# Routing of a mixture-of-experts layer: splits on one engine, the norm's root ahead of the last rows, the gates' table ahead of the gathered rows, two experts in a written order

## The chip, the core and the metric

One core of a Trainium2 chip runs the kernel. Its engines run side by side and wait for each other by semaphores: TensorE (PE) multiplies matrices, VectorE (DVE) and ScalarE (ACT) work on whole tiles, GpSimd (POOL) works on tiles and issues the transfers with computed addresses, SyncE (SP) issues most plain transfers. The metric is the device time of one execution in microseconds.

## The reference

A decoder layer with 1024 tokens of width 1024. A mixing part and a cross-attention to a memory come first, and both add to `x`. Then comes the mixture of experts, with which this document deals: of 4 groups with 8 experts each a token takes the best group, and in it the two best experts.

```python
pg = softmax(t @ w_rg + b_rg); gate_g, gidx = top_k(pg, 1)
el = (t @ w_re + b_re).reshape(N, 4, 8)[arange(N), gidx]
pe_top, eloc = top_k(softmax(el), 2)
wts = gate_g * pe_top / sum(pe_top)
# for each expert e and the rows xb that chose it
y = (silu(xb @ w_gate[e]) * (xb @ w_up[e])) @ w_down[e]
out = einsum('nk,nkd->nd', wts, y)
x = x + out;  return rms_norm(x, norm_final)
```

`t` is the RMS norm of `x`, with the gain `norm_ffn`. All is float32.

## The kernel before, in words

**Products in three terms.** A float32 operand is split into a high part (`whi`, a cast on ACT, L285) and a low part (`wlo`, the difference, L286). A product is three matrix products: high by high (L141), low by high (L142), high by low (L143).

**The weights' stream.** `plan` lists all weight tiles in the order of their use, 512 KB each. `pump()` loads tiles on SP's queue up to `ahead["load"]` tiles ahead of the use, and splits them up to `ahead["split"]` tiles ahead. `take()` hands out the next tile and calls `pump()`. An expert uses 12 tiles: 4 of `w_gate`, 4 of `w_up`, 4 of `w_down`. While experts run the load is 30 and 31 tiles ahead, from expert 16 on only 10 (`LF`, `EF`). Raw tiles, their halves, the gathered rows, `y` and more share one pool of 45 buffers (`unit`). A scheduler deals them out, by its own simulation, when the program is built; a tile that gets a buffer waits for whoever used it before.

**The end of the memory stage (`mem_out`, `tail`, `mem_end`).** The tokens lie in two halves (`hf`) and the features in 8 slices (`f`). For each slice `fin` adds the last product to `x2`, and `tail` multiplies `x2` into the routing logits (`plg`), transposes it (`pt`), writes the rows times gain (`rowg`, DVE) and the plain rows (`rows`, ACT), and stores both from ACT's queue, to `td` (read by the gathers) and `x2d` (to which the experts add). After the last slice `rsq` computes the norm's root from `plg`, in 11 small DVE instructions (L157 to L165).

**Routing (`route`).** DVE finds the group and the experts, PE counts ranks (L1113 to L1118), DVE builds one-hot matrices (`Rb`, `R`, `V`), PE turns them into the list of tokens of each expert (`idx`, L1146 and L1152). POOL then issues the gathers of experts 0, 1 and 2 (`xg<-td,idx`). A second product, `table` (L1182, 16 matrix instructions), gives the gates `tab`; for `hf == 1` it is put off (`late`).

**Experts.** `x_t(e)` transposes the gathered rows on PE (`px`) and splits them (`xth` on ACT, `xtl` on DVE). `gate_up(e)` is 48 products with 512 columns, `h_t(e)` four transposes and a split (`ht`), `down(e)` 24 products and the scaled copy `y`; POOL adds `y` to `x2d` by a scatter with addition (L1415). `down(e - 1)` runs in the turn of expert `e`. Ahead of expert 0 stand `x_t(0)`, the gather of expert 3, the table and a count of blocks (8 small products, L1425, and 14 small DVE instructions, L1428 to L1435), which only the rare overflow blocks need.

**Order.** SP and POOL run in the order of the code throughout. PE, DVE and ACT are in code order from the last slice to the end of `route`; after that the scheduler orders them.

Of the kernel before, what the change touches and what calls it, by code (L numbers as in the profile page):

```python
# [12 lines left out]
AF = mybir.ActivationFunctionType  # L13
OP = mybir.AluOpType
AX = mybir.AxisListType
# [4 lines left out]
D = 1024  # L20
KT = 8
H = 512
NE = 32
# [22 lines left out]
RM = {mybir.EngineType.DVE, mybir.EngineType.PE, mybir.EngineType.Activation}  # L46
# [24 lines left out]
PS = 4  # L71
# [43 lines left out]
def tile_layer(tc, a, out):  # L115
    nc = tc.nc
# [7 lines left out]
    mm = nc.tensor.matmul  # L124
# [6 lines left out]
    def half(name, shape=(128, H), dt=F32):  # L131
        return up.tile(list(shape), dt, name=name, tag="v", bufs=NV)

    def ps1(name="ps"):
        return psum.tile([128, 512], F32, name=name, tag="ps", bufs=4)
# [877 lines left out]
        for i in range(2):  # L1013
            nc.gpsimd.memset(Mb[i][:, 0:3], 0.0)

    late = []

    def load_gfb():
        gfb["t"] = unit("gfb", [128, D])
        row(gfb["t"], a["norm_ffn_row"], D)  # L1020
# [22 lines left out]
    def route(hf, pl, store):  # L1043
# [105 lines left out]
        if hf == 0:  # L1149
            nc.vector.tensor_scalar(tabi, pt[:, :NE], 8192.0, None, op0=OP.add)  # L1150
        else:
            tt(idx, tabi, pt[:, :NE], op=OP.add)  # L1152
            for e in range(NX):
                gather(e)
            store(x2d, KT - 1)
            ahead["lo"] = nc.vector
        gs = tl("gs", N)
        red(gs, ge, axis=AX.X, op=OP.add)
        gate = tl("gate", N)
# [28 lines left out]
                tt(tf, tf, pt[:, :64], op=OP.add)  # L1188

        if hf:  # L1190
            late.append(table)
        else:
            table()
            yield 1.8, 0.0
# [8 lines left out]
    def mem_out(hf):  # L1203
        hs = slice(hf * H, (hf + 1) * H)
        plg = ps1("plg")
        rows = [None, None]

        def store(dst, f, i=0):
            nc.scalar.dma_start(dst[hs, (f - 1) * 128:(f + 1) * 128].rearrange("(t p) c -> p t c", p=128), rows[i])

        def zero_mm(start, stop):
            mm(plg[:, :168], oneb[0:1], bc(Mb[0][0:1, 0, None, 0:28], [1, 6, 28]), start=start, stop=stop)


        zero_mm(True, False)
        pend = []

        def logit(f, x2):
            for t in range(4):
                mm(plg[:, t * 36:t * 36 + 36], x2[:, t * 128:(t + 1) * 128], wr[:, f], start=False, stop=False)  # L1220

        def tail(f, x2):
            fs = slice(f * 128, (f + 1) * 128)
            if f < KT - 1:
                logit(f, x2)
            else:
                logit(f, x2)
                for t in range(4):
                    mm(plg[:, 160 + 2 * t:162 + 2 * t], acc["x2", hf][1][:, t * 128:(t + 1) * 128], ones[:, 0:2],
                       start=False, stop=False)  # L1230
                zero_mm(False, True)
            pt = ps1("pt")
            for t in range(4):
                nc.tensor.transpose(pt[:, t * 128:(t + 1) * 128], x2[:, t * 128:(t + 1) * 128], ident)

            if f % 2 == 0:
                rows[0] = unit("rows", [128, 4, 256])
                rows[1] = unit("rowg", [128, 4, 256])
            cs = slice((f % 2) * 128, (f % 2 + 1) * 128)
            p3 = pt.rearrange("p (t c) -> p t c", t=4)  # L1240
            tt(rows[1][:, :, cs], p3, bc(gfb["t"][:, None, fs], [128, 4, 128]), op=OP.mult)
            nc.scalar.copy(rows[0][:, :, cs], p3)
            if f % 2:
                store(td, f, 1)
                if not (hf and f == KT - 1):
                    store(x2d, f)
            if f == KT - 1:
                rsq(r3[:, 4 * hf:4 * hf + 4], plg[:, 160:168:2], D, 1e-6, "r")

        def fin(f, p, x2):  # L1250
            tt(x2, x2, p, op=OP.add)
            colsum(("x2", hf), x2, f)
            if pend:
                tail(*pend.pop())
            pend.append((f, x2))

        grp = {}
        todo = [(f, 0, 8) for f in range(KT)]
        if hf == 0:
            todo = [(0, 0, 6), (1, 0, 6), (0, 6, 8), (1, 6, 8)] + todo[2:]  # L1260
        for f, k0, k1 in todo:
            if k0 == 0:
                x2 = half("x2")
                nc.sync.dma_start(x2, x1d[f * 128:(f + 1) * 128, hs])
                if hf:
                    ahead["load"] += PF
                grp[f] = (take(), ps1("pp"), x2)
            (wh, wl), p, x2 = grp[f]
            for k in range(k0, k1):
                if k == 6:  # L1270
                    for x in until(("om", 3, hf)):
                        yield x
                if (f, k) == (7, 5):
                    for t in range(4):
                        mm(plg[:, 160 + 2 * t:162 + 2 * t], acc["x2", hf][0][:, t * 128:(t + 1) * 128], ones[:, 0:2],
                           start=False, stop=False)
                o = om[k, hf]
                mm3(p, wh[:, k], wl[:, k], o[:, 0], o[:, 1], k == 0, k == KT - 1)
                if k in (1, 3, 5):
                    yield 1.28, 0.0  # L1280
            if k1 == 8:
                fin(f, p, x2)
                yield 1.28, 0.0
        for k in range(KT):
            om.pop((k, hf))
        fini[hf] = (lambda: tail(*pend.pop())), plg, store
        done.add(("mo", hf))

    def mem_end(hf):
        for x in until(("mo", hf)):  # L1290
            yield x
        last, plg, store = fini[hf]
        if hf:
            man = tc.manual_schedule(engines=RM)
            man.__enter__()
        else:
            yield 0.0, 0.8
        last()
        if hf:
            for i in range(NX):  # L1300
                xg.append(unit("xg", [128, D]))
                nc.gpsimd.memset(xg[i], 0.0)
            ahead["load"] += PG
            ahead["lo"] = nc.gpsimd
            ahead["split"] = PS
            pump()
        yield 2.0, 3.0
        for x in route(hf, plg, store):
            yield x
        if hf:  # L1310
            man.__exit__(None, None, None)
# [61 lines left out]

    hts = {}

    def gate_up(e):
        xh, xl = xts.pop(e)
        gu = []
        for w in range(2):
            p = ps1("pgu")  # L1380
            for q in range(4):
                wh, wl = take()
                for k2 in range(2):
                    k = 2 * q + k2
                    ks = slice(k * 128, (k + 1) * 128)
                    mm3(p, xh[:, ks], xl[:, ks], wh[:, k2], wl[:, k2], k == 0, k == KT - 1)
            gu.append(p)
        hh = half("hh")
        nc.scalar.activation(hh, gu[0], AF.Silu, scale=tab[:, 1, e:e + 1])
        nc.vector.scalar_tensor_tensor(hh, gu[1], tab[:, 1, e:e + 1], hh, op0=OP.mult, op1=OP.mult)  # L1390
        hts[e] = hh
# [10 lines left out]
    def down(e):  # L1402
# [8 lines left out]
        if e == NE - 1:  # L1411
# [4 lines left out]
                                     in_=y, in_offset=None, bounds_check=S - 1, oob_is_err=False,  # L1416
                                     compute_op=OP.add)

    x_t(0)
    gather(NX)  # L1420
    late[0]()
    op = ctx.enter_context(tc.tile_pool(name="ov", bufs=1))
    pc = ps1()
    for t in range(8):
        mm(pc[:, :NE], oneb, Mb[t // 4][:, 3 + t % 4], start=(t == 0), stop=(t == 7))  # L1425
    nb = op.tile([128, NE], F32, name="nb")
    t1 = op.tile([128, NE], F32, name="t1")
    nc.vector.tensor_scalar(nb, pc[:, :NE], 128.0, None, op0=OP.is_gt)  # L1428
    for j in range(2, 8):
        nc.vector.tensor_scalar(t1, pc[:, :NE], 128.0 * j, None, op0=OP.is_gt)  # L1430
        nc.vector.tensor_add(nb, nb, t1)
    nov = op.tile([128, 2], F32, name="nov")
    nc.vector.tensor_reduce(nov[:, 0:1], nb, axis=AX.X, op=OP.add)
    novi = op.tile([128, 1], I32, name="novi")
    nc.vector.tensor_copy(novi, nov[:, 0:1])  # L1435
    for e in range(NE):
        ahead["load"] = LF if e >= NE - EF else max(LE, LA - LD * e)
        if e >= NE - ES:
            ahead["split"] = LZ
        if e >= NE - ED:  # L1440
            down(e - 1)
        gate_up(e)
        if e + 1 < NE:
            x_t(e + 1)
        if e + 1 + NX < NE:
            gather(e + 1 + NX)
        if 0 < e < NE - ED:
            down(e - 1)
        h_t(e)
        if e == 4:  # L1450
            nr = nc.values_load(novi[0:1, 0:1], min_val=0, max_val=NOV - 1,
                                skip_runtime_bounds_check_because="2048 assignments leave at most 15 further blocks")
        if e == PK:
            gfin = unit("gfin", [128, D])
            row(gfin, a["norm_final"], D)
# [221 lines left out]
```

## Time and profile before

| What | us |
|---|---|
| median of 3 runs (1419.73 to 1422.47) | 1420.8 |
| the profiled execution's own time | 1421.64 |
| its span, from the first to the last instruction | 1419.9 |
| PE busy in it | 1324.5 |
| DVE busy in it | 1006.7 |
| ACT busy in it | 832.9 |
| last weight product of the memory stage, last slice's logits | until 770 |
| first product of expert 0 starts | 797.38 |
| last product of the weights ahead of the final norm | ends about 1388 |

Times within the span are counted from its start. An idle time in a row stands in square brackets, with what ended it. PE's span between about 770 and 797 is where routing leaves it nearly idle; the profile's row of the granted clock shows 0.5 there.

### The profile page before, as it was taken

The page shows a single profiled execution, that of the slowest core. Times are in us where ns is not written, and L with a number is a line of the kernel's source. Part 1 is how long each engine was busy: PE and PEld are TensorE (multiplying, and loading weights), DVE is VectorE, ACT ScalarE, POOL GpSimd, SP SyncE. Part 2 cuts the span into 40 slices and gives each one's busy share as a digit, 9 for nine tenths or more (in the row PEclk, how much of TensorE's full clock was granted, in tenths as well). Part 3 has the DMA queues.
Part 4 walks back from the last instruction along what each step waited for, and adds up shares of the span by engine and source line. Part 5 has one row for each costly group of instructions (what it writes and reads, how often), then busy time and mean ns, then how long its engine had stood idle before and what let it go on. Part 6 is the DMA issues. An engine that isn't in the chain of part 4 may idle for free.

```text
span 1419.9 us, 20537 instructions
## 1 busy us (share of the span) xinstructions
PE 1324.5 (93%) x7420; PEld 1147.9 (81%) x7420; DVE 1006.7 (71%) x1593; ACT 832.9 (59%) x1136; POOL 263.9 (19%) x289
## 2 busy tenths in 40 slices
PE   7889999999999999999997799999989999999980
PEld 5889898989887889999886578888778888888860
DVE  6746685667856444333365778999879999999975
ACT  7524563455545553333222478888868888888863
POOL 3231210311112331112114101111111111111012
PEclk9989999999999999999998799999999999999995
DMA  8540211212275665013699599999999699999985
GB/s 308 157 133 1 60 45 60 83 45 46 82 241 184 203 230 180 16 46 102 231 329 336 189 325 356 363 355 357 354 369 349 241 369 381 371 355 370 369 285 205
DMA packets 103225, 322.39 MB, mean 227 GB/s; under 512 B 15747, under 2 KB 23971, under 8 KB 103120
## 3 DMA queue, kind: packets, MB, share of 16 engines
q1 hardware_dynamic: 76896, 272.14, 52.3%
q0 software_dynamic: 17776, 40.51, 10.3%
q10 hardware_dynamic: 8448, 8.39, 1.7%
q8 instruction: 59, 0.97, 0.3%
q14 instruction: 46, 0.38, 0.1%
HBM read 287.10 MB, written 46.66 MB: 235 GB/s over the span
## 4 chain that ended last, share of the span: by engine, by line
PE 69%; DMA 15%; DVE 7%; issue 5%; ACT 3%; POOL 1%; SPq 0%; POOLq 0%; ACTq 0%; DVEq 0%
PE pp L141 11%; PE pp L142 11%; PE pp L143 11%; PE pgu L142 5%; PE pgu L143 5%; PE pgu L141 5%; DMA raw<-in_w_gate 4%; DMA raw<-in_w_down 4%; DMA raw<-in_w_up 3%; PE py L141 3%; PE py L143 3%; PE py L142 3%; PE px L1369 1%; DVE wlo L286 1%; DMA x2d<-y,idx 1%
## 5 line engine op out<-in xcount | busy, mean ns | idle before, releaser
L286 DVE TENSOR_TENSOR wlo<-raw,whi 128x1024 fp32r<-128x1024 f32 (+1 forms) x467 | 553.9, 1225 | 87.0 <-ACT whi L285 77.4
L285 ACT CAST whi<-raw 128x1024 fp32r<-128x1024 f32 (+1 forms) x469 | 471.9, 1049 | 67.3 <-PE pgu L142 11.0
L141 PE MATMUL pgu<-whi,xth 128*128 128x512 f32 x512 | 198.5, 396 | 6.1 <-ACT whi L285 6.1
L142 PE MATMUL pgu<-wlo,xth 128*128 128x512 f32 x512 | 201.5, 394 | 1.4 <-DVE wlo L286 1.4
L143 PE MATMUL pgu<-whi,xtl 128*128 128x512 f32 x512 | 201.1, 393 | 0.3 <-DVE xtl L147 0.3
L1415 POOL DMA_INDIRECT x2d<-y,idx x31 | 49.6, 1600 | 462.8 <-ACT y L1414 419.4
L141 PEld LDWEIGHTS pgu<-whi,xth 128*128 128x128 f32 x512 | 97.0, 189 | 27.6 <-ACT whi L285 8.2
L142 PEld LDWEIGHTS pgu<-wlo,xth 128*128 128x128 f32 x512 | 96.9, 189 | 22.9 <-DVE wlo L286 2.3
L143 PEld LDWEIGHTS pgu<-whi,xtl 128*128 128x128 f32 x512 | 97.0, 189 | 20.6 <-DVE xtl L147 0.7
L141 PE MATMUL py<-whi,ht 128*128 128x512 f32 x256 | 102.4, 400 | 4.8 <-ACT whi L285 2.5
L142 PE MATMUL py<-wlo,ht 128*128 128x512 f32 x256 | 103.6, 405 | 0.4 <-DVE wlo L286 0.4
L143 PE MATMUL py<-whi,ht 128*128 128x512 f32 x256 | 101.1, 395 | 0.0
L639 ACT ACTIVATE p<-p,stt 128x128 f32<-128x128 f32 (+7 forms) x64 | 49.6, 776 | 49.9 <-DVE stt L638 40.7
L142 PE MATMUL pp<-wlo,hTh 128*128 128x256 f32 x256 | 73.1, 285 | 1.5 <-DVE wlo L286 1.5
L141 PE MATMUL pp<-whi,hTh 128*128 128x256 f32 x256 | 73.5, 287 | 0.2 <-ACT whi L285 0.2
L141 PE MATMUL pp<-whi,h2h 128*128 128x256 f32 x256 | 73.1, 285 | 0.0
L143 PE MATMUL pp<-whi,hTl 128*128 128x256 f32 x256 | 72.9, 285 | 0.0
L142 PE MATMUL pp<-wlo,h2h 128*128 128x256 f32 x256 | 72.5, 283 | 0.0
L143 PE MATMUL pp<-whi,h2l 128*128 128x256 f32 x256 | 72.5, 283 | 0.0
L141 PE MATMUL pp<-hTh,whi 128*128 128x512 f32 x160 | 64.4, 403 | 0.4 <-ACT ot L691 0.4
L143 PE MATMUL pp<-hTh,wlo 128*128 128x512 f32 x160 | 63.5, 397 | 0.0
L142 PE MATMUL pp<-hTl,whi 128*128 128x512 f32 x160 | 63.5, 397 | 0.0
(361 smaller groups left out, 2963.4 us busy)
## 6 DMA issues: line engine op xcount, KB each, us to landing
raw<-in_w_gate SPq DMA_DIRECT2D x128, 512.0 KB
raw<-in_w_up SPq DMA_DIRECT2D x128, 512.0 KB
raw<-in_w_down SPq DMA_DIRECT2D x128, 512.0 KB
raw<-in_w_in SPq DMA_DIRECT2D x19, 512.0 KB
raw<-in_w_kv_mem SPq DMA_DIRECT2D x16, 512.0 KB
raw<-vwd SPq DMA_DIRECT2D x16, 512.0 KB
raw<-in_w_q_memT SPq DMA_DIRECT2D x8, 512.0 KB
raw<-in_w_out SPq DMA_DIRECT2D x8, 512.0 KB
```

Of the source, the lines that this page charges most:

```text
L141: mm(o, sh, mh, start=start, stop=False)
L142: mm(o, sh, ml, start=False, stop=False)
L143: mm(o, sl, mh, start=False, stop=stop)
L285: nc.scalar.copy(hi[:, c], raw[:, c])
L286: ahead.get("lo", nc.vector).tensor_tensor(lo[:, c], raw[:, c], hi[:, c].bitcast(F32), op=OP.subtract)
L639: nc.scalar.activation(pe[:, :nk], pe[:, :nk], AF.Exp, bias=stt[:, 2 + m:3 + m], scale=slopes[hd], accum_out=stt[:, 4 + m:5 + m])
L1369: nc.tensor.transpose(px[:, k * 128:(k + 1) * 128], x[:, k * 128:(k + 1) * 128], ident)
L1415: nc.gpsimd.indirect_dma_start(out=x2d[:, :], out_offset=bass.IndirectOffsetOnAxis(ap=idx[:, e:e + 1], axis=0), in_=y, in_offset=None, bou ...
```

## The change

Five edits, in `tail`, `mem_end`, `route` and the start of the expert loop:

- `rsq` runs as soon as the logits are complete, ahead of the last slice's transposes. For the last slice of the second half ACT makes a copy of `x2` scaled by the gain (`x2g`), PE transposes this copy first and `x2` after it, and ACT writes both results; DVE's multiplication is gone there.
- The setting that sent the low parts to POOL (`ahead["lo"]`) goes; DVE does all. The four-tile-ahead split is raised at the end of `route`, not at its start.
- `table()` runs at the end of `route`, ahead of `x_t(0)`.
- The order of PE, DVE and ACT stays as written through experts 0 and 1. There `h_t(0)` stands between the two products of `gate_up(1)`.
- The count of blocks moves behind expert 1.

```diff
-            ahead["lo"] = nc.vector
...
         if hf:
-            late.append(table)
+            ahead["split"] = PS
+            pump()
+            table()
...
+            if f == KT - 1:
+                rsq(r3[:, 4 * hf:4 * hf + 4], plg[:, 160:168:2], D, 1e-6, "r")
...
+            if hf and f == KT - 1:
+
+                x2g = half("x2g")
+                nc.scalar.activation(x2g, x2, AF.Copy, scale=gffn[:, f:f + 1])
+                nc.scalar.copy(rows[1][:, :, cs], turned(x2g))
+                store(td, f, 1)
+                nc.scalar.copy(rows[0][:, :, cs], turned(x2))
+                return
+            p3 = turned(x2)
             tt(rows[1][:, :, cs], p3, bc(gfb["t"][:, None, fs], [128, 4, 128]), op=OP.mult)
...
-            if f == KT - 1:
-                rsq(r3[:, 4 * hf:4 * hf + 4], plg[:, 160:168:2], D, 1e-6, "r")
...
             ahead["load"] += PG
-            ahead["lo"] = nc.gpsimd
-            ahead["split"] = PS
             pump()
...
             gu.append(p)
+            if w == 0 and between:
+                between()
...
+    man = tc.manual_schedule(engines=RM)
+    man.__enter__()
     x_t(0)
     gather(NX)
-    late[0]()
...
-        gate_up(e)
+        gate_up(e, between=(lambda: h_t(0)) if e == 1 else None)
...
-        h_t(e)
+        if e:
+            h_t(e)
+        if e == 1:
+            man.__exit__(None, None, None)
+            count_blocks()
```

`turned(x)` is the four transposes that stood there before; `count_blocks()` holds the count as it was.

On DVE, at the last slice and the root, before (`x_7412` is the last slice's `x2`, `w_r` the root's scratch):

```order
L286 TENSOR_TENSOR wlo<-raw,whi 128x1024
L1241 TENSOR_TENSOR rowg<-pt,gfb 128x4x128
L1251 TENSOR_TENSOR x_7412<-x_7412,pp 128x512
L1241 TENSOR_TENSOR rowg<-pt,gfb 128x4x128
L157 TENSOR_SCALAR w_r<-plg 128x4
L158 TENSOR_SCALAR w_r<-w_r 128x4
L161 SCALAR_TENSOR_TENSOR w_r<-w_r 128x4
```

and now:

```order
L286 TENSOR_TENSOR wlo<-raw,whi 128x1024
L1253 TENSOR_TENSOR rowg<-pt,gfb 128x4x128
L1260 TENSOR_TENSOR x_7412<-x_7412,pp 128x512
L157 TENSOR_SCALAR w_r<-plg 128x4
L158 TENSOR_SCALAR w_r<-w_r 128x4
L161 SCALAR_TENSOR_TENSOR w_r<-w_r 128x4
```

The last `rowg` multiplication, which waits for transposes, no longer stands ahead of the root. POOL's two low parts of this place now stand on DVE behind `R`.

On PE, from the token lists to the first product of expert 0, before (`Rb` and `R` are the one-hot matrices, `px` the gathered rows turned, `cb` the ones of the count):

```order
L1146 MATMUL ps<-V,Rb 128x32
L1362 MATMUL px<-ident,xg 128x128 x8
L1182 MATMUL ps<-V,R 128x64 x8
L1425 LDWEIGHTS cb
L1425 MATMUL ps<-Mb_102,cb 128x32
```

and now:

```order
L1144 MATMUL ps<-V,Rb 128x32
L1179 MATMUL ps<-V,R 128x64 x8
L1369 MATMUL px<-ident,xg 128x128 x8
L141 MATMUL pgu<-whi,xth 128x512
L142 MATMUL pgu<-wlo,xth 128x512
```

The table stands ahead of the gathered rows, and nothing is left between these and the first product.

On ACT, in the turn of expert 2, with buffer numbers and waits, before (`y_7989` is expert 0's `y`; its scatter with addition signals `DMASW4`):

```order
L285 CAST whi_8029<-raw_7418 128x1024 [waits DVE_49,PE_49]
L285 CAST whi_8041<-raw_7420 128x1024 [waits DMAHW6_49,DVE_49]
L1389 ACTIVATE hh_8100<-pgu_8002,tab_96 128x512 [waits PE_49]
L285 CAST whi_8054<-raw_7518 128x1024 [waits DMAHW7_49,DMASW4_49]
L285 CAST whi_8066<-raw_7520 128x1024 [waits DMAHW0_49,PE_49]
```

and now:

```order
L285 CAST whi_8039<-raw_7418 128x1024 [waits DVE_49]
L285 CAST whi_8051<-raw_7420 128x1024 [waits DMAHW6_49,DVE_49]
L1398 ACTIVATE hh_8110<-pgu_8012,tab_96 128x512 [waits PE_49]
L285 CAST whi_8064<-raw_7525 128x1024 [waits DMAHW7_49]
L285 CAST whi_8076<-raw_7527 128x1024 [waits DMAHW0_49,PE_49]
```

The cast of the eighth tile no longer waits for expert 0's scatter: the buffers are dealt out another way. The buffer of expert 0's `y` now goes to `raw_8062`, a load for expert 4 on SP's queue.

## Rows read from the trace of the kernel before

**Rows 1.** Chain of waits, late experts: start us, us, what.
```profile
1250.37 0.23 PE py L142
...
1250.71 14.40 DMA raw<-in_w_gate
```
**Rows 2.** Table by stretches: stretch, length, busy times, clock, DMA share, GB/s.
```profile
771.00:778.00 7.00, 0.42 (x4) 0.26 (x3) 6.62 (x12) 2.48 (x3) 4.63 (x2) 0.50 1.01 348
```
**Rows 3.** PE in order of time, routing: start us, us, instruction, idle before.
```profile
769.63 0.32 PE L1212 MATMUL plg<-Mb,cb 1*128 1x168 bf16 x1
...
792.08 1.94 PE L1362 MATMUL px<-ident,xg 128*128 128x128 f32 x8 [5.56 <-DMA xg<-td,idx]
793.81 3.52 PE L1182 MATMUL ps<-V,R 128*128 128x64 f32 x16
...
797.38 0.77 PE L141 MATMUL pgu<-whi,xth 128*128 128x512 f32 x1
...
798.80 0.63 PE L141 MATMUL pgu<-whi,xth 128*128 128x512 f32 x1
...
800.08 0.44 PE L141 MATMUL pgu<-whi,xth 128*128 128x512 f32 x1
```
**Rows 4.** DVE in order of time, routing and count.
```profile
771.64 0.15 DVE L157 TENSOR_SCALAR w_r<-plg 128x4 f32<-128x4 f32 x1
...
773.21 0.16 DVE L161 SCALAR_TENSOR_TENSOR w_r<-w_r 128x4 f32<-128x4 f32 x1
773.41 2.32 DVE L162 TENSOR_TENSOR w_r<-w_r 128x4 f32<-128x4 f32 x1
775.76 2.26 DVE L165 SCALAR_TENSOR_TENSOR r<-w_r 128x4 f32<-128x4 f32 x1
...
788.55 1.22 DVE L1173 TENSOR_TENSOR R<-ra,rk 128x1024 f32<-128x1024 f32 x1
...
797.68 0.18 DVE L1430 TENSOR_SCALAR t<-ps 128x32 f32<-128x32 f32 x1
```
**Rows 5.** POOL in order of time, routing and first experts.
```profile
773.37 4.63 POOL L286 TENSOR_TENSOR wlo<-raw,whi 128x1024 fp32r<-128x1024 f32 x2 [7.94 <-ACT whi L285]
787.58 1.14 POOL L1039 DMA_INDIRECT xg<-td,idx  x1 [9.57 <-DVE wsel L1164]
...
834.30 1.36 POOL L1039 DMA_INDIRECT xg<-td,idx  x1 [0.31 <-issue]
```
**Rows 6.** ACT's queue in order of time: the last store to `td`.
```profile
771.77 0.37 ACTq L1209 DMA_DIRECT2D td<-rowg  x1
```
**Rows 7.** Tile `td`, 690 to 830 us, 12 transfers.
```profile
DMA to landing us min/median/max: 4.1/4.8/7.5
```
**Rows 8.** Tiles `xth` and `xtl` in the experts: ns min/median/max, first and last start.
```profile
L146 ACT CAST xth<-px x31: 999/1008/1020, 810.9 to 1351.7; 128x1024 fp32r<-128x1024 f32 x31
L147 DVE TENSOR_TENSOR xtl<-px,xth x31: 1214/1217/1226, 811.9 to 1353.0; 128x1024 fp32r<-128x1024 f32 x31
```
**Rows 9.** PE in order of time, experts.
```profile
813.18 0.50 PE L143 MATMUL pgu<-whi,xtl 128*128 128x512 f32 x1 [0.31 <-DVE xtl L147]
...
843.08 0.50 PE L141 MATMUL pgu<-whi,xth 128*128 128x512 f32 x1 [2.88 <-ACT whi L285]
...
866.26 0.39 PE L142 MATMUL py<-wlo,ht 128*128 128x512 f32 x1
```
**Rows 10.** ACT in order of time, experts 2 and 3.
```profile
841.98 3.89 ACT L285 CAST whi<-raw 128x1024 fp32r<-128x1024 f32 x4 [4.43 <-DMA x2d<-y,idx]
...
863.28 1.06 ACT L285 CAST whi<-raw 128x1024 fp32r<-128x1024 f32 x1 [0.58 <-PE pgu L142]
865.00 1.05 ACT L285 CAST whi<-raw 128x1024 fp32r<-128x1024 f32 x1 [0.66 <-DMA x2d<-y,idx]
```
**Rows 11.** Table by stretches, behind PE's stop at 843.
```profile
844.00:848.00 4.00, 3.97 (x10) 3.07 (x11) 3.83 (x5) 3.58 (x4) 0.00 (x0) 0.57 0.85 314
```
**Rows 12.** What SP's queue waited for, 1085 to 1120: us, times, longest.
```profile
SPq L276 <- DVE wlo L286: 19.8, 5, 16.5
```

More of the change, by code (lines that the diff above doesn't have):

```diff
@@ L1014, in small_consts @@
             nc.gpsimd.memset(Mb[i][:, 0:3], 0.0)
-    late = []
     def load_gfb():
@@ L1231, in tail, with turned @@
                 zero_mm(False, True)
-            pt = ps1("pt")
-            for t in range(4):
-                nc.tensor.transpose(pt[:, t * 128:(t + 1) * 128], x2[:, t * 128:(t + 1) * 128], ident)
+            if f == KT - 1:
+                rsq(r3[:, 4 * hf:4 * hf + 4], plg[:, 160:168:2], D, 1e-6, "r")
+            def turned(x):
+                pt = ps1("pt")
+                for t in range(4):
+                    nc.tensor.transpose(pt[:, t * 128:(t + 1) * 128], x[:, t * 128:(t + 1) * 128], ident)
+                return pt.rearrange("p (t c) -> p t c", t=4)
             if f % 2 == 0:
@@ L1239, in tail @@
             cs = slice((f % 2) * 128, (f % 2 + 1) * 128)
-            p3 = pt.rearrange("p (t c) -> p t c", t=4)
+            if hf and f == KT - 1:
[6 more added lines that the diff above has]
+            p3 = turned(x2)
             tt(rows[1][:, :, cs], p3, bc(gfb["t"][:, None, fs], [128, 4, 128]), op=OP.mult)
@@ L1244, in tail @@
                 store(td, f, 1)
-                if not (hf and f == KT - 1):
-                    store(x2d, f)
-            if f == KT - 1:
-                rsq(r3[:, 4 * hf:4 * hf + 4], plg[:, 160:168:2], D, 1e-6, "r")
+                store(x2d, f)
         def fin(f, p, x2):
@@ L1374, in tile_layer, with gate_up @@
     hts = {}
-    def gate_up(e):
+    def gate_up(e, between=None):
         xh, xl = xts.pop(e)
@@ L1417, in down, with count_blocks @@
                                      compute_op=OP.add)
+    man = tc.manual_schedule(engines=RM)
+    man.__enter__()
     x_t(0)
     gather(NX)
-    late[0]()
     op = ctx.enter_context(tc.tile_pool(name="ov", bufs=1))
-    pc = ps1()
-    for t in range(8):
-        mm(pc[:, :NE], oneb, Mb[t // 4][:, 3 + t % 4], start=(t == 0), stop=(t == 7))
     nb = op.tile([128, NE], F32, name="nb")
     t1 = op.tile([128, NE], F32, name="t1")
[L1428 to L1431, printed above, removed]
     nov = op.tile([128, 2], F32, name="nov")
-    nc.vector.tensor_reduce(nov[:, 0:1], nb, axis=AX.X, op=OP.add)
     novi = op.tile([128, 1], I32, name="novi")
-    nc.vector.tensor_copy(novi, nov[:, 0:1])
+    def count_blocks():
+        pc = ps1()
+        for t in range(8):
+            mm(pc[:, :NE], oneb, Mb[t // 4][:, 3 + t % 4], start=(t == 0), stop=(t == 7))
+        nc.vector.tensor_scalar(nb, pc[:, :NE], 128.0, None, op0=OP.is_gt)
+        for j in range(2, 8):
+            nc.vector.tensor_scalar(t1, pc[:, :NE], 128.0 * j, None, op0=OP.is_gt)
+            nc.vector.tensor_add(nb, nb, t1)
+        nc.vector.tensor_reduce(nov[:, 0:1], nb, axis=AX.X, op=OP.add)
+        nc.vector.tensor_copy(novi, nov[:, 0:1])
     for e in range(NE):
```

## The prediction

> **What bounds the kernel now.** I read the chain of waits from its end backwards first. From 1250 us on it runs through transfers of weights, and at 1250.71 it turns into a product of an expert's `w_down` [rows 1]: late loads start when a product gives up a buffer, so an earlier PE makes them earlier. Further back, in the experts, products follow each other every 0.23 us [rows 1], and an expert's 72 take some 17 us. PE sets the pace there, with few stops. That leaves two things to look at: those stops, and the stretch in which PE stands for want of lists. For this I read PE, DVE, POOL and ACT in order of time between 770 and 798. PE's last logits end at 769.95, its gathered rows come at 792.08, expert 0 starts at 797.38 [rows 3], and the clock granted in the beginning of this stretch is 0.50 [rows 2]. The chain runs over DVE (root, ranks, lists), POOL (gather), a transfer and PE. Whatever shortens it moves everything behind, loads included.
>
> The sum is made against the profiled execution's 1421.64 us; the median of the runs is 1420.8, which is 0.84 less. About 0.2%, 2.8 us, is what a measurement of this kernel can tell from no change.
>
> **The change part by part.** *The root ahead.* DVE starts the root at 771.64 [rows 4], since the last `rowg` multiplication stands ahead of it and waits for transposes. The logits are there at 769.63 + 0.32 = 769.95 [rows 3]. With that multiplication gone the root starts at about 770.0: **-1.6**. What took its place (a scaled copy, a second turn, two ACT copies) lies on ACT and PE, which have nothing else to do till the ranks. What hides it is judged below, at the store of `td`.
>
> *Low parts on DVE alone.* Two of the root's small instructions last 2.32 and 2.26 us, their neighbour on the same tile 0.16 [rows 4]. Just then, from 773.37, POOL makes two low parts in 4.63 us, 2.3 each [rows 5]. The long ones stood for as long as one of POOL's. On DVE's own queue low parts can't do that: (2.32 - 0.16) + (2.26 - 0.16) = **-4.3**. The two low parts now lie behind `R`, 2 x 1.22 us (the length of `R`, of the same shape [rows 4]). Nothing there waits for them before the first product, and DVE is idle meanwhile.
>
> Together -5.9: the first gather goes from 787.58 [rows 5] to 781.7, the end of `R` from 788.55 + 1.22 = 789.77 [rows 4] to 783.9.
>
> *The table ahead of the gathered rows.* Before, 792.08 to 797.38 are 5.3 us from the first turned rows to the first product, with the table's 3.52 within [rows 3]. The rows would now be there at 792.08 - 5.9 = 786.2, but the table starts with `R`, at 783.9, and ends at 787.4: it holds the rows up by 1.2. Behind it only the first half of the turn (some 1.0 of its 1.94 [rows 3]), its cast (half of 1.008 [rows 8]) and handovers remain, 2.0 in all. First product at 787.4 + 2.0 = 789.4 instead of 797.38: **-8.0** for the three edits together, -2.1 of it from the table. The low clock of the first products I leave as it was: products get short at 800.08 [rows 3], 8 us behind the first turn and 2.7 behind the first product, and PE now starts its table 5.5 us ahead of expert 0, nearly as the 5.3 before.
>
> *The written order of experts 0 and 1.* The scheduler had mixed the turn of expert 1 and `h_t(0)` between products; PE waited 0.31 us for `xtl` [rows 9]. In the written order nothing stands between the turn of expert 1 and its first product: PE waits for `xth`, 1.0 us and a handover, 1.1, and after two products for `xtl`, 1.22 less 0.46 [rows 8, 1], 0.75. That is 1.85 - 0.3 = **+1.5** (0 if the scheduler's mix cost as much elsewhere; 1.7 more if the clock falls).
>
> *The count behind expert 1.* 14 DVE instructions of 0.18 [rows 4], 2.5 us, and eight products of under 0.1 us now stand in expert 1 or 2, where the scheduler fits them between; before, they lay where DVE had little else. **+0.5** (0 to +2.8).
>
> *The buffers.* In the turn of expert 2 ACT waited 4.43 us for expert 0's scatter [rows 10]; PE stood 2.88 for the cast behind it [rows 9] and went on at a clock of 0.57 for 4 us [rows 11], which loses 4 x 0.43 = 1.7. The new deal of buffers lets that cast wait for its load alone: -2.88 - 1.7 = **-4.6** (0 to -5). That buffer now goes to a load for expert 4. SP will stand at it till the scatter lands, about as long as ACT would have stood and a little more, 7 us; some 30 tiles of lead cover it, and if they don't, that is the first rival.
>
> The deal turns against the kernel in two places. In expert 3's turn the first tile of `w_down`, cast at 863.28, now waits for expert 1's scatter, as the second does at 865.00 [rows 10]. PE needs that tile's low part about when it now multiplies it, 866.26 [rows 9]; cast and low part end at 865.0 + 1.05 + 1.22 = 867.3 and a handover later, so **+1.2**. One more such wait appears in the turn of expert 14, behind expert 12's scatter: **+1.2** again (each 0 to +3.4, the upper end with 1.7 for the clock as above). The last norm I leave at 0 (-1 to +1.5).
>
> Sum: -8.0 + 1.5 + 0.5 - 4.6 + 1.2 + 1.2 = -8.2. From 1421.64 that is 1413.4, and against the median **1412.6**. With the smaller terms at either end I hold 1409.5 to 1415.5 for this case.
>
> **The rivals.** *The stream takes the buffers' part back.* SP's queue now stands 7 us, and the faster experts use 4.6 us of the stream's slack. The slack shows where the lead is cut at expert 16: 16.5 us of waiting in one piece [rows 12]. That is more than 11.6, which speaks against it; that transfers are close to full beside expert 2 (0.85 [rows 11]) speaks for it. Then the 4.6 come back: 1417.2.
>
> *Slower: the clock.* The written order makes PE stop for 1.1 and 0.75 us at the start of expert 1, and no other work fills it. A stop of 2.88 took the clock to 0.57 [rows 9, 11]. If PE, coming out of routing, doesn't rise to the full clock before these stops and falls again at them, its 72 products up to expert 1's `up` part run 0.43 apart, as the three from 798.80 to 800.08 [rows 3], not 0.23. The first six, up to 800.08, did so before. (72 - 6) x 0.2 = +13.2: 1425.8. It decides from the point at which stops this short count as the long one did. In its favour is only that PE did start low before; against it, that its products got short 2.7 us behind the first.
>
> The Trainium skill ("TensorE: Matmul & The Clock Gate", section "A second HAM failure mode: psum-queue depth-cycling") speaks for this rival: it tells of a kernel in which frequent short idle times between groups of products, none of them long, made the clock swing. By it the time would be this rival's, 1425.8. No row above shows such short stops in a series, so the trace neither agrees nor speaks against it.
>
> *The gather gains nothing.* The last store to `td` is issued at 771.77 [rows 6] and now, behind two ACT copies, at about the same time. Transfers there land after 4.8, at most 7.5 us [rows 7], so at 779.3, 2.4 ahead of the new gather. All engines of the DMA are busy there (1.01 [rows 2]). With a landing of 12 us the gather would wait 2.4: 1415.0, and 1 us for each further one.
>
> *Better.* The two new waits and the written order cost nothing: 1412.6 - 3.9 = 1408.7.
>
> **How the numbers follow.** Forecast 0.62; stream 0.13, of which 0.05 beyond 1418.0; gather 0.07; better 0.08; the clock 0.05; several small terms at their dear ends, about 1418 to 1420, 0.05. Range: 1407.0 to 1418.0, which leaves out the clock, the dear ends and part of the stream's. Faster by over 0.2% (below 1418.0): 0.62 + 0.08 + 0.07 + 0.08 = 0.85. Within 0.2%: 0.10. Slower: 0.05.
>
> **What would show it.** In the new trace: the root's start near 770.0 and all its instructions near 0.16; the first gather near 781.7; table ahead of turn, first product near 789.4; PE idle some 1.1 and 0.75 at expert 1's start, clock full behind it; no stop at expert 2's eighth tile; in the turns of experts 3 and 14 stops of about 1 us that end with a cast behind a scatter; SP idle at expert 16 for less than 16.5. It is wrong if the gather waits for `td`, if DVE's long instructions stay long without POOL, or if PE waits for loads.

## The result, and the profile after

| | before | changed |
|---|---|---|
| median, us | 1420.8 (5 runs, 1416.82 to 1422.47) | 1409.82 (5 runs, 1408.05 to 1411.39) |
| span of the profiled execution | 1419.9 | 1408.1 |
| first product of expert 0 | 797.38 | 789.12 |
| last expert product ends (its start and 0.23, the step from product to product) | 1387.75 | 1379.67 |
| from there to the end of the span | 32.15 | 28.43 |

The changed kernel takes 0.992 of the time of the kernel before (95% interval 0.9907 to 0.9932). That is faster by more than 0.2%, inside the range of 1407.0 to 1418.0, and 2.8 us below the predicted 1412.6. One run of the kernel with the root alone (below) took 1683.64 us at a granted clock of 0.741, and no number here contains it.

The routing came out as in the sum, almost to the tenth. DVE in order of time (start us, us, instruction, idle before), which answers to [rows 4]:

```profile
769.99 0.16 DVE L157 TENSOR_SCALAR w_r<-plg 128x4 f32<-128x4 f32 x1 [2.45 <-PE plg L1211]
...
770.58 0.16 DVE L162 TENSOR_TENSOR w_r<-w_r 128x4 f32<-128x4 f32 x1
770.78 0.16 DVE L165 SCALAR_TENSOR_TENSOR w_r<-w_r 128x4 f32<-128x4 f32 x1
...
782.57 1.22 DVE L1170 TENSOR_TENSOR R<-ra,rk 128x1024 f32<-128x1024 f32 x1
783.71 2.35 DVE L286 TENSOR_TENSOR wlo<-raw,whi 128x1024 fp32r<-128x1024 f32 x2
```

The root starts 0.04 behind the last logits, all its steps last 0.16, and the two low parts lie behind `R`. POOL, against [rows 5]:

```profile
781.67 1.14 POOL L1037 DMA_INDIRECT xg<-td,idx  x1 [15.95 <-DVE wsel L1161]
783.12 1.57 POOL L1037 DMA_INDIRECT xg<-td,idx  x1 [0.30 <-issue]
```

And PE, against [rows 3]:

```profile
783.94 3.65 PE L1179 MATMUL ps<-V,R 128*128 128x64 f32 x16 [3.32 <-DVE R L1170]
787.38 1.92 PE L1369 MATMUL px<-ident,xg 128*128 128x128 f32 x8
789.12 0.76 PE L141 MATMUL pgu<-whi,xth 128*128 128x512 f32 x1
789.71 0.40 PE L142 MATMUL pgu<-wlo,xth 128*128 128x512 f32 x1
```

No idle time stands between the table, the turn and the first product. But the second product is already at its short length; before, six were slow. The experts, against [rows 9]:

```profile
802.56 0.50 PE L141 MATMUL pgu<-whi,xth 128*128 128x512 f32 x1 [1.10 <-ACT xth L146]
...
803.82 0.50 PE L143 MATMUL pgu<-whi,xtl 128*128 128x512 f32 x1 [0.53 <-DVE xtl L147]
...
853.13 0.50 PE L141 MATMUL py<-whi,ht 128*128 128x512 f32 x1 [0.16 <-ACT whi L285]
...
854.39 0.50 PE L142 MATMUL py<-wlo,ht 128*128 128x512 f32 x1 [0.76 <-DVE wlo L286]
...
1032.23 0.79 PE L141 MATMUL pgu<-whi,xth 128*128 128x512 f32 x1 [2.26 <-ACT whi L285]
...
1033.50 0.80 PE L142 MATMUL pgu<-wlo,xth 128*128 128x512 f32 x1 [0.47 <-DVE wlo L286]
...
1058.75 0.50 PE L142 MATMUL py<-wlo,ht 128*128 128x512 f32 x1 [0.69 <-DVE wlo L286]
```

The stops at expert 1 are there, expert 2 has none, the two new waits stop PE at 853 and at 1058, and the old stop of expert 13 is still there. The first of the new waits is ACT's, for expert 1's scatter:

```profile
852.02 2.00 ACT L285 CAST whi<-raw 128x1024 fp32r<-128x1024 f32 x2 [2.54 <-DMA x2d<-y,idx]
```

The other one stands the same way at 1056.38, after 1.77 of waiting.

What the sum didn't hold is the end: the way from the last product to the end of the span is 3.7 shorter.

### The profile page after: what moved, and what is told of

Same layout as the page of the kernel before. It is cut to its first block, busy times and chain, and to the rows that moved or that the text cites. A ratio compares the mean times of both kernels' runs of the same rounds, so it can differ in the third digit from the quotient of the medians.

```text
span 1408.1 us, 20553 instructions
## 1 busy us (share of the span) xinstructions
PE 1325.6 (94%) x7424; PEld 1148.1 (82%) x7424; DVE 1001.1 (71%) x1594; ACT 833.9 (59%) x1138; POOL 262.0 (19%) x287
```

## The experiments

In the records PE's first expert product is a good mark; so is the way from the root's start on DVE to the first gather on POOL, since it doesn't depend on when the memory stage ended in that record. That way is 15.94 us in the kernel before and 11.68 in the changed one.

But for its second record the changed kernel didn't run beside the experiments; each has a ratio to the kernel before from its own session. By these ratios the late table (0.9939, 0.9923 to 0.9956), the count first (0.9939, 0.9922 to 0.9955) and the end without POOL (0.990, 0.9884 to 0.9917) can't be told from the changed kernel with certainty, since their intervals overlap its 0.9907 to 0.9932. What is said of these three rests on the positions in the traces.

**The low parts alone.** The kernel before, with the split raised behind `R` and no low part on POOL:

```diff
+            ahead["split"] = PS
+            pump()
             late.append(table)
...
-            ahead["lo"] = nc.gpsimd
-            ahead["split"] = PS
             pump()
```

> The kernel before with one edit: the two low parts of the routing stand on VectorE behind R, as in the changed kernel; root, table, order and count stay. Theory (the root's two long instructions stood for POOL's two low parts): all eleven instructions of the root take 0.16 to 0.2, the first gather is issued 4.3 earlier than in the kernel before, at about 783.3, the first product of expert 0 at about 793.1, the time falls by about 4.3, to 1416.5. Rival (the root's instructions are long for another reason, such as the transfers beside them): they stay at 2.3 and the time stays within 1 of 1420.8.

Median 1416.05, ratio 0.9962 (0.9948 to 0.9976). Root to gather 783.21 - 771.53 = 11.68, first product at 793.02. The two steps of 2.3 are gone with POOL's work: the theory stands, at 4.3 us.

**The low parts ahead of the routing.** As above, but the split stays where the kernel before has it:

```diff
-            ahead["lo"] = nc.gpsimd
```

> As the run before it, but the two low parts stand on VectorE between the root and the routing's first step, where the kernel before gave them to POOL. Theory: 4.3 of POOL's hindrance are saved and 2 x 1.22 of VectorE's own work are put in, so the first gather comes 1.9 earlier than in the kernel before, at about 785.7, and the time is about 1418.9, between the kernel before and the run with the low parts behind R. Rival: the saving is the same as in that run, 4.3, since VectorE has waits there to fill.

Root to gather 785.36 - 771.54 = 13.82. DVE's record shows why:

```profile
773.58 2.35 DVE L286 TENSOR_TENSOR wlo<-raw,whi 128x1024 fp32r<-128x1024 f32 x2
```

2.35 of DVE's own work stand on the chain in place of 4.3 of waiting, and the first product (795.26) is 2.12 earlier than before, as expected. So half of the edit's gain hangs on where the split was moved to. The median, 1416.66 (0.9971, 0.9958 to 0.9983), fell further than the 1418.9 of the theory and can't be told from that of the low parts alone. In the profiled execution the rest lies at the end of the kernel, which takes 29.6 from the last product instead of 32.15 (below).

**The root alone.** The kernel before, with `rsq` ahead of the transposes:

```diff
+            if f == KT - 1:
+                rsq(r3[:, 4 * hf:4 * hf + 4], plg[:, 160:168:2], D, 1e-6, "r")
             pt = ps1("pt")
...
-            if f == KT - 1:
-                rsq(r3[:, 4 * hf:4 * hf + 4], plg[:, 160:168:2], D, 1e-6, "r")
```

> The kernel before with one edit: the root stands ahead of the last rows' transposes and multiplication; POOL keeps its low parts. Theory (what collides with POOL's low parts is whatever small two-operand step of VectorE stands there at that time): the root starts at 770.0 and is short throughout, but instructions of the routing behind it now last about 2.3, twice; the multiplication of 0.7 stands behind the root, so the first gather is only 0.9 earlier, 786.7, and the time about 1420. Rival (only the root is hurt): the gather is 1.6 + 4.3 - 0.7 = 5.2 earlier, 782.4, and the time about 1415.6.

The root is short, and the long steps have moved on. DVE, then POOL:

```profile
773.61 2.16 DVE L1073 TENSOR_TENSOR r_ao<-r_ae,r_af 128x128 f32<-128x128 f32 x1
775.69 2.31 DVE L1073 TENSOR_TENSOR r_go<-r_ge,r_gf 128x16 f32<-128x16 f32 x1
```

```profile
773.28 4.69 POOL L286 TENSOR_TENSOR wlo<-raw,whi 128x1024 fp32r<-128x1024 f32 x2 [9.61 <-ACT whi L285]
```

Root to gather is 785.03 - 768.90 = 16.13, no shorter than before. What is hurt isn't the root but a DVE step that stands beside POOL's. That the root itself starts earlier shows against the last logits on PE:

```profile
768.54 0.32 PE L1212 MATMUL plg<-Mb,cb 1*128 1x168 bf16 x1
```

From their end to the gather it is 785.03 - 768.86 = 16.17, and it was 787.58 - 769.95 = 17.63 before: 1.5 of the 1.6 that the sum gives to the root. Median 1418.81 (0.9987, 0.9977 to 0.9997).

**The low parts back on POOL.** The changed kernel with that edit undone:

```diff
             store(x2d, KT - 1)
+            ahead["lo"] = nc.vector
...
-            ahead["split"] = PS
-            pump()
             table()
...
             ahead["load"] += PG
+            ahead["lo"] = nc.gpsimd
+            ahead["split"] = PS
             pump()
```

> The changed kernel with one edit undone: the routing's low parts are on POOL again, split at the place of the kernel before. Theory: two small instructions of VectorE between 773 and 779 last about 2.3 instead of 0.2 to 0.3, the first gather is issued at about 786.0 instead of 781.67, the first product of expert 0 at about 793.4 instead of 789.12, and the time is about 4.3 over the changed kernel's, 1414.1. Rival (the gain came from the root's place alone): the gather stays at 781.7 and the time at 1409.8.

DVE's long steps come back, on still other instructions:

```profile
773.47 2.32 DVE L1069 TENSOR_TENSOR r_ge<-r_ge,desc 128x16 f32<-128x16 f32 x1
...
776.02 2.19 DVE L1071 TENSOR_TENSOR r_ao<-r_ae,r_af 128x128 f32<-128x128 f32 x1
```

Root to gather 785.36 - 769.67 = 15.69, 4.0 more than in the changed kernel; median 1415.26, 5.4 more, against 4.3 in the theory. In the profiled execution slow products account for more than that difference: 1.0 at the start of expert 0 and 1.6 at expert 1 (below).

**The table late again.** The changed kernel with `table()` behind `x_t(0)`:

```diff
-            table()
+            late.append(table)
...
     gather(NX)
+    late[0]()
```

> The changed kernel with one edit undone: the table stands behind the turn of expert 0's rows again, in the written order. Theory: the rows come at about 786.2, their turn starts there, the table runs behind it and holds the first product to about 791.5 instead of 789.12; the first products are slow as in the kernel before (0.43 apart, six of them, 1 us in all); the time is about 2.4 to 3.4 over the changed kernel's, 1412.2 to 1413.2. Rival (the first products are fast whatever the order, since PE's work ahead of them lasts as long): only the 2.4 show.

Median 1412.37, 2.6 over the changed kernel. In PE's record the rows' turn comes first and the table holds the product up:

```profile
786.16 1.94 PE L1370 MATMUL px<-ident,xg 128*128 128x128 f32 x8 [5.61 <-DMA xg<-td,idx]
787.89 3.52 PE L1179 MATMUL ps<-V,R 128*128 128x64 f32 x16
791.16 0.77 PE L141 MATMUL pgu<-whi,xth 128*128 128x512 f32 x1
```

That is 2.04 by the first product; ten products were slow from there on. The rows came 786.16 - 781.62 = 4.5 behind the gather's issue, as before (792.08 - 787.58), so the gather didn't wait for the store of `td`.

**No written order.** The changed kernel without `manual_schedule` at experts 0 and 1:

```diff
-    man = tc.manual_schedule(engines=RM)
-    man.__enter__()
...
-            man.__exit__(None, None, None)
             count_blocks()
```

> The changed kernel without the written order of experts 0 and 1: the scheduler orders them, and deals the buffers anew. It puts the turns of experts 1 and 2 ahead of the first product of expert 0. Theory: PE then waits for the gather of expert 2, which lands at about 790, so that the first product comes at about 791.5 instead of 789.1; the stops of 1.10 and 0.53 at expert 1 are gone; the scatter of expert 0 holds a cast of expert 2 again and costs PE 3 to 4.6; the time is 1412 to 1416. Rival (the written order costs more than it gives, as my sum has it, +1.5): the time is about 1408.3.

Median 1419.68 (ten runs, 1416.9 to 1422.12), above the 1412 to 1416 of the theory: nearly the whole gain is gone. The profiled execution, with a span of 1415.2, is the fastest of the ten. PE:

```profile
790.86 1.10 PE L1376 MATMUL px<-ident,xg 128*128 128x128 f32 x8 [1.31 <-DMA xg<-td,idx]
791.71 0.48 PE L141 MATMUL pgu<-whi,xth 128*128 128x512 f32 x1
...
803.72 0.50 PE L141 MATMUL pgu<-whi,xth 128*128 128x512 f32 x1 [0.83 <-ACT xth L146]
...
805.39 0.50 PE L143 MATMUL pgu<-whi,xtl 128*128 128x512 f32 x1 [0.94 <-DVE xtl L147]
...
835.32 0.79 PE L141 MATMUL pgu<-whi,xth 128*128 128x512 f32 x1 [3.38 <-ACT whi L285]
```

The scheduler put the turns of experts 1 and 2 ahead of the first product, and PE waited for a gather that it didn't need yet. The stops at expert 1 are not gone, as the theory had it, and no shorter than in the written order, and expert 0's scatter holds a cast of expert 2 again. The rival falls: with the table early, the scheduler's order costs more than the written one. How much of it is order and how much the deal of buffers stays open, since both changed.

**The count first.** The changed kernel with `count_blocks()` ahead of the loop:

```diff
+    count_blocks()
     for e in range(NE):
...
             man.__exit__(None, None, None)
-            count_blocks()
```

> The changed kernel with one edit undone: the count of blocks stands ahead of expert 0 again, in the written order. The deal of buffers then lets a cast of expert 2 wait for expert 0's scatter again. Theory (the count itself is cheap, what counts is the deal): the first product comes at most 0.5 later than 789.12, PE stands about 2.9 at the eighth tile of expert 2 and runs slow for 4 us behind it, and the time is about 4 to 5 over the changed kernel's, 1414 to 1415. Rival (the count was the cost, on VectorE ahead of expert 0's low parts): PE stops in expert 0 for 2 to 3 and not in expert 2.

Median 1412.58, 2.8 over the changed kernel, less than expected. The first product is at 789.03, 19.43 behind the root's start against 19.13 in the changed kernel, so the count costs 0.3 there. Expert 2 stops again, by its deal of buffers. ACT, then PE:

```profile
835.95 3.90 ACT L285 CAST whi<-raw 128x1024 fp32r<-128x1024 f32 x4 [3.69 <-DMA x2d<-y,idx]
```

```profile
837.04 0.50 PE L141 MATMUL pgu<-whi,xth 128*128 128x512 f32 x1 [1.66 <-ACT whi L285]
...
837.99 0.49 PE L141 MATMUL py<-whi,ht 128*128 128x512 f32 x1 [0.45 <-ACT whi L285]
```

The mechanism holds, the size was smaller: 2.11 of standing instead of 2.9, and no slow stretch behind it. The profiled execution, 1415.09, is the slowest of the four; the clock fell in it behind the stops of expert 1.

**Buffers of its own for `y`.** Two, with 43 in the shared pool, and one, with 44:

```diff
-NU = 45
+NU = 43
...
-        y = unit("y", [128, D])
+        y = up.tile([128, D], F32, name="y", tag="y", bufs=2)
```

> The changed kernel with a change of its own: the experts' y has two buffers of its own, and the shared pool has 43 instead of 45, so that no cast of weights waits for a scatter. Theory: the stops of 0.92 in expert 3's turn, of 2.73 with a slow stretch behind in expert 13's and of 0.69 in expert 14's are gone, about 6 us in all, and the time is about 1404. Rival (two buffers less leave the loads too late): SP's waits grow, PE waits for loads, and the time is 1410 or more.

> The changed kernel with one buffer of its own for y and 44 instead of 45 in the shared pool, to part what the run with 43 mixed: no cast waits for a scatter, and one buffer less. Theory (with 43 the cost was the missing buffers, 0.6 an expert, and the late end of the memory stage, 2.2): half of that or none is left, the stops at experts 3, 13 and 14 are gone, and the time is between 1404 and 1414. Rival (any buffer less costs 0.6 an expert and more): 1418 or more.

1421.69 and 1435.71: no gain in either, as the rivals had it (1410 or more, 1418 or more). The stops behind scatters are gone and others came. What SP's queue waited for between 860 and 1080 (us in total, times, longest), in the changed kernel:

```profile
SPq L276 <- PE pgu L143: 20.8, 29, 1.2
...
SPq L276 <- DVE wlo L286: 5.5, 10, 0.9
```

and with 43 buffers:

```profile
SPq L276 <- PE pgu L143: 42.4, 37, 2.0
...
SPq L276 <- DVE wlo L286: 35.6, 38, 1.7
```

Both also end the memory stage later; the root starts at 772.24 and 773.25 instead of 769.99. Then loads wait for buffers to be given back. With 43 the theory's 6 us did come back, 0.9 at expert 3 and 5.7, with the slow stretch, at experts 12 and 13. But in every expert from 4 to 10 PE loses 0.6 on the way from its gate to its up products, and from 21 to 28 it loses 1.2 an expert. Why 44 and one come out worse than 43 and two isn't settled. There PE also stood for `hh` and `xtl` on DVE, up to 1.8 at a time, and one `y` had to wait 8.0 for the scatter ahead of it; the casts behind it on ACT stopped PE for 6.46.

**The end without POOL.** The changed kernel with DVE scaling all rows of the last norm:

```diff
-FP = (3, 5, 7)
+FP = ()
```

> The changed kernel with a change of its own at the end: the three multiplications by the final gain that GpSimd made for rows 3, 5 and 7 are gone, and VectorE scales these rows by root and gain in one step, as it does the others. Theory (GpSimd's tile-long steps hold VectorE's small steps of the last root for 2.3 each, at the end as in the routing): the two small steps of 2.31 are down to 0.16, 4.3 saved, against 3 x 1.27 of rows that VectorE now scales itself; from the last product's end to the end of the span 27 to 28.5 instead of 28.4, the time 1408 to 1410. Rival (these steps are long for another reason): they stay, and the time is 3 to 4 over the changed kernel's, 1413.

Median 1406.7 (0.990 of the kernel before), the lowest of all and below the 1408 to 1410 expected. At the end of the changed kernel POOL and DVE look like the old routing; POOL first:

```profile
1384.49 5.24 POOL L1626 TENSOR_TENSOR xf<-xf,gfin 128x1024 f32<-128x1024 f32 x2 [3.13 <-ACT xfs L1624]
```

```profile
1385.13 2.31 DVE L161 SCALAR_TENSOR_TENSOR w_f<-w_f 128x1 f32<-128x1 f32 x1
...
1387.44 2.31 DVE L157 TENSOR_SCALAR w_f<-rfin 128x2 f32<-128x2 f32 x1
```

Without POOL's steps the same part of DVE reads

```profile
1385.08 0.15 DVE L161 SCALAR_TENSOR_TENSOR w_f<-w_f 128x1 f32<-128x1 f32 x1
...
1385.22 0.16 DVE L157 TENSOR_SCALAR w_f<-rfin 128x2 f32<-128x2 f32 x1
```

and the end, from the last product, takes 25.89 instead of 28.43, though DVE scales three more rows. That is more than the theory's own sum, 4.3 less 3 x 1.27. DVE is done only 0.7 earlier (17.0 behind the last product instead of 17.7); the rest lies behind it, where the last scatter on POOL follows DVE's end by 3.7 instead of 5.5. The last two stores in between were issued 0.4 apart in the changed kernel and 1.2 apart here; no run tests whether that is why they took longer there.

**Both kernels again.** The same programs, for second records.

> The changed kernel as it is, for another record of the same program. Theory (when the clock rises in expert 0, and whether it falls at the stops of 1.10 and 0.53 at expert 1, changes from run to run of the same instructions): the first product starts at 789.1 again and PE stops again for 1.10 and 0.53, but the number of slow first products differs from 1, or a slow stretch of 3 to 4 us stands behind the stops. Rival (order and stops decide it): one slow product and no slow stretch, as in the first record. Time 1408 to 1412.

> The kernel before as it is, for another record. Theory (the order of VectorE's small steps at the end, which the build sets, makes the end long): three small steps of 2.3 to 2.5 behind the last product again, the last gathered rows' step 1.5 to 4 behind the last product, 29.5 to 32.5 from the last product to the end, against 28.4 in the changed kernel. Rival (the long end of the first record was an accident of its transfers): under 29.

1408.89 and 1420.36. In the second record of the changed kernel the first product is at 787.77, since the memory stage ended 1.3 earlier (the root starts at 768.66). The stops at expert 1 are again 1.10 and 0.53, but six products were slow at the start of expert 0, and the clock fell behind the stops. By stretches (length, busy times, granted clock, DMA share, GB/s), first record and second:

```profile
803.00:805.00 2.00, 1.48 (x7) 1.00 (x6) 2.00 (x3) 1.47 (x3) 0.00 (x0) 1.00 0.91 311
805.00:807.00 2.00, 2.00 (x11) 1.64 (x10) 1.84 (x2) 1.57 (x2) 0.00 (x0) 1.00 0.77 254
```

```profile
803.00:805.00 2.00, 1.51 (x5) 1.21 (x6) 1.91 (x3) 1.47 (x3) 0.00 (x0) 0.80 1.00 350
805.00:807.00 2.00, 2.00 (x6) 1.51 (x6) 0.89 (x1) 0.65 (x1) 0.00 (x0) 0.50 0.61 176
```

At expert 13 it is the other way round: in the first record the clock is at 0.50 from 1032 to 1038, behind the stop, in the second it stays at 1.00. So neither when the clock rises nor whether a stop takes it down is set by the program alone. The kernel before shows three long steps at its end in both records:

```profile
1389.21 2.33 DVE L162 TENSOR_TENSOR w_f<-w_f 128x2 f32<-128x2 f32 x1
...
1391.66 1.28 DVE L1613 SCALAR_TENSOR_TENSOR xg<-py,tab,xg 128x1024 f32<-128x1024 f32 x1
...
1396.32 2.39 DVE L165 SCALAR_TENSOR_TENSOR w_f<-w_f 128x2 f32<-128x2 f32 x2
...
1398.70 2.45 DVE L161 SCALAR_TENSOR_TENSOR w_f<-w_f 128x2 f32<-128x2 f32 x3
```

(x2 and x3 are rows of several steps, of which one is long.) The step `xg<-py,tab,xg`, which takes the last product's result, stands on DVE behind one of them and starts 3.91 behind that product (1.6 in the second record). In the changed kernel it stands ahead of them:

```profile
1379.86 1.28 DVE L1630 SCALAR_TENSOR_TENSOR xg<-py,tab,xg 128x1024 f32<-128x1024 f32 x1 [3.62 <-PE py L143]
```

This is an order that the scheduler makes, and it goes with no single edit: the kernel before, the low parts alone, the root alone, the late table and the kernel without a written order have three long steps (29.3 to 32.2 from the last product to the end, 30.4 on average over six records), the other kernels, but for the one without POOL, have two (28.4 to 29.6, 28.8 over seven).

## Why the prediction held, and where it was off

In the profiled executions the span fell by 11.8, the sum said 8.2. The terms that the sum holds came to -9.6 together. The end, -3.7, and the clock, +1.6, lay outside it, and that they partly cancel is luck. Step by step, with the positions of the same product in both records:

| step | predicted | measured |
|---|---|---|
| root, low parts, table: first product | -8.0 | -8.26 |
| clock at expert 0's first products | 0 | -1.0 |
| written order | +1.5 | +1.3 |
| count | +0.5 | +0.3 |
| expert 0's scatter | -4.6 | -5.0 |
| expert 1's scatter | +1.2 | +0.9 |
| expert 12's scatter | +1.2 | +1.2 |
| clock behind expert 13's stop | 0 | +1.0 |
| experts 28 to 31 | 0 | -0.25 |
| clock at the last 24 products | 0 | +1.6 |
| from the last product to the end | 0 | -3.7 |

The written order is 1.10 + 0.53 less the 0.31 of [rows 9]; expert 0's scatter is 2.88 + 0.44 of standing and 1.7 at the low clock; expert 1's is 0.16 + 0.76. The count is what remains between the first product and expert 4, where the changed kernel is 11.75 ahead. Expert 12's is what is lost between the gate products of experts 14 and 16 (10.68 to 9.44 ahead).

**Right, and shown.** The root's long steps stood for POOL's low parts: they go with POOL's work (low parts alone), come back with it (low parts back), and move to another instruction when the root moves (root alone). By the first gather the low parts' place is worth 4.3 (low parts alone) and the root's place 1.5 (root alone). That the edit is worth 4.3 and not 1.9 depends on the later split (low parts ahead). The Trainium skill ("SBUF — State Buffer", section "🔬 SBUF: two separate sides") tells of a port pair that VectorE and GpSimd share as an exclusive lock, the loser waiting for the whole instruction of the other; these records agree, with one small DVE step of 2.16 to 2.32 for each POOL step of 2.3 in the routing. The table was worth 2.0 by the first product (late table), 2.1 in the sum. That a cast of expert 2 waited by the deal of buffers, and that moving the count changed this deal, is shown by the count put back; 2.11 of standing there, so -4.6 was the price in this record and not a fixed one.

**Mis-sized: the end.** The term that was off is the last one, "the last norm I leave at 0 (-1 to +1.5)"; it measured -3.7. The prediction looked for POOL beside DVE in the routing alone. The same thing stands at the end: POOL multiplies three rows by the final gain, and in the order of before `xg<-py,tab,xg` stands behind a small step that lasted 2.33 beside one of these (DVE's 1389.21, above):

```profile
1389.19 2.33 POOL L1609 TENSOR_TENSOR xf<-xf,gfin 128x1024 f32<-128x1024 f32 x1 [7.27 <-ACT xfs L1607]
```

From the start of `xg<-py,tab,xg` to the end of the span it is 28.2 to 28.3 in both records of both kernels. So the whole 3.7 is the later start of this step: 3.91 behind the last product before (1.6 in the second record), 0.19 in the changed kernel (1.3 in the second record, where it waited for the gathered rows). Of the 3.91, 2.2 is the long step, and 1.4 is DVE's wait ahead of it for a sum of squares on ACT, whose row had come late from `x2d`. By the averages above the order is worth 1.7; the rest is within what two records of one program differ by (32.15 and 29.94). The kernel without POOL at the end shows that the changed kernel's long steps stand for POOL's. No run took POOL from the end of the kernel before, so its 2.2 are read from these rows and not tested.

**Not in the sum, and not the change's: the clock.** Its three entries, -1.0, +1.0 and +1.6, add up to +1.6. They belong to the records, as the second record of the changed kernel shows.

**The rivals.** The stream took nothing back. SP stood 5.4 at expert 0's scatter (7 in the prediction), and where the lead is cut, in the same stretch as [rows 12], it still had more slack:

```profile
SPq L276 <- DMA x2d<-y,idx: 5.4, 1, 5.4
```

```profile
SPq L276 <- DVE wlo L286: 23.4, 5, 19.8
```

The slack grew, against the sign that the prediction names: less than 16.5 was expected, 19.8 came (16.9 in the second record). The gather gained all that the root gave (late table, 4.5 from issue to rows as before). Its rival was also priced too high: a landing of 12 us ends at 783.8 and holds the gather by 2.1, not by 2.4, and the table covers 1.2 of that. The slow clock came, but not as feared: in the second record and in the runs with the low parts back, the count first and one buffer for `y` it fell behind the stops of expert 1; in the first record and with the late table it didn't. In the run with the low parts back the gate products of expert 1 took 8.35 instead of 6.74, so one fall costs 1.6, and no record shows it lasting over 72 products. The Trainium skill ("TensorE: Matmul & The Clock Gate", section "What's actually happening") says of the slow products at a start that their number is "run-variable"; one and six of them in the two records of the changed kernel agree.

The written order was costed at +1.5 against the scheduler's order of before. With the other edits in place that isn't the alternative: the scheduler then stops PE by 0.83 and 0.94 at the same place and by 1.31 ahead of expert 0 (no written order).

## What to carry to other kernels

Where a step of a few columns lasts as long as a whole tile, look for the engine that has a tile-long step at the same time, and look for it in every stage: the same remedy was worth 4.3 in the routing, and 2.5 more at the end, 0.7 of it on DVE itself. An edit that moves a few small instructions can re-deal a shared pool or re-order a far stage, so compare all waits of both builds, and don't give their gain to the edit. To move work off an engine is half the gain; where its new place stands on the chain is the other half (2.35 of 4.3 here).

## What the runs showed of the hardware

The same program with the same stops of 1.10 and 0.53 us kept the clock at 1.00 in one record, and in another it fell to 0.50 behind them; a fall cost 1.6 us. The time from PE's first work behind the routing to its first short product was between 5.8 and 9.4 us in the fourteen records. It was 5.8 and 7.9 in two records of one program, so I read no rule for the order of that work from it.

In the routing, and at the end of the kernel before, one small DVE step was long for each POOL step on a tile (2.16 to 2.35). In the changed kernel the first of POOL's three steps at the end (1379.00, 2.36) lies beside `xg<-py,tab,xg`, which reads `py` from PSUM and kept its 1.28, and the small step behind it took only 0.32. Steps with two tensors as operands were hit, and at the end also a `TENSOR_SCALAR` of 128x2 with one (2.31). A `TENSOR_REDUCE` beside POOL's second low part kept its 0.15 (low parts back, 775.91).
